# First block: own buffers for the modulation weights, an even split of the convolution taps, and another order of the output projection

## The chip, the cores and the metric

The program runs on one core of a Trainium2 chip. The metric is the device time of one execution in microseconds, and the median of a few executions is compared. The core's engines have a queue each: TensorE (PE, with its weight loads shown apart as PEld), VectorE (DVE), ScalarE (ACT), GpSimd (POOL) and SyncE (SP), which starts the large transfers from memory. Each queue runs in order. What one engine needs from another it waits for at a semaphore.

## The reference, cut to what matters

The program is two networks in a row. Only the first is touched, and a set of vectors that the second needs. The first has two layers over 272 rows (16 meta tokens and 256 tokens) of width 1024:

```
hn = rmsnorm(h, norm1_g[l]);  proj = hn @ w_in[l]          # q, k, v, u
q, k = rope(q), rope(k)
attn = rmsnorm((softmax(q1 k1) - lam * softmax(q2 k2)) @ v, subln_g) * (1 - lam_init)   # 4 heads
z    = a * sigmoid(gate)                                   # a, gate from u + b_glu
conv = silu(layer_norm(depthwise_conv(z, 31 taps) + conv_b))    # 512 channels
h = h + concat(attn, conv) @ w_out[l]
h = h + (silu(gate) * up) @ w_down[l]
```

The second network scales and shifts its rows by modulation vectors, silu(c) @ w_ada + b_ada, of 6 x 1024 values. They depend on no row of the first network, so they may be computed at any time before.

## The kernel before

Activations lie transposed, channels on partitions and rows along the free axis. A weight matrix is read in blocks of 1024 x 256 (1 MB). `weights` (L153) puts a block into one of three `raw` buffers by a transfer from SP's queue, then ACT and DVE split it into a high and a low half (`hi`, `lo`, three buffers each), and `mm3` (L169) takes three products of reduced precision for each 128 x 128 piece.

In each layer `first_block` makes z from four blocks of w_in (L352 to L365), q and k from four more (L372 to L386), v from two (`values`), and then attention, convolution and the output projection. `ORDER` gives the order in which the source lists the steps: scores, values, attention, convolution, part of the modulation (`ada_parts`), the channel norm, and the four blocks of w_out. The source's order is not the order on the engines: a planner with a model of the times lists each engine's instructions, and an earlier place in the source is a higher priority. `high_priority` raises it.

The rows of the attention are cut into three tiles of 16, 128 and 128 rows (two in the second layer, which drops the first). `scores` makes one product for each tile, head and half (L420), adds the mask and takes the maximum on DVE (L421), exponentiates on ACT (L425), and joins the two halves on DVE (L428 to L431). `attention` transposes the weights (L453), multiplies with v (L461), and norms each tile by itself: four squares on ACT (L465), a root, a reciprocal, a product (L470), transposes (L474), and the split into `cat` (L477, L478).

The convolution has 31 taps for each of four groups of 128 channels. `TAPS` says which run on TensorE: in the first layer all 31 of group 0 and 16 of group 1, in the second 16 of group 0. Such a tap needs a diagonal matrix made by ACT (L487) and is one product (L488). The others are one DVE instruction each (L498, L501). `channel_norm` follows, with sigmoid written by Tanh (L521).

The modulation has 24 parts of 256 columns, 12 in the first layer, 10 in the second and 2 after the last w_down (`ADA`). Each takes 1 MB of w_ada through a `raw` buffer (the last two through the buffers `xh` and `xl`, `ada_ahead`), eight products with 32 columns (L630), a copy on ACT (L633) and two products that turn the row (L635). The buffer `bigb` holds `cat` from early in the layer on, and later half of the MLP's activations.

The output projection keeps five accumulators open (`AHEAD`), takes for them the half of w_out that meets the attention first, then the half that meets the convolution.

Of the kernel before, what the change touches and what calls it, by code (L numbers as in the profile page):

```python
# [13 lines left out]
OP = mybir.AluOpType  # L14

# [12 lines left out]
ADA = (12, 10, 2)  # L28
TAPS = (((0, 31), (1, 16)), ((0, 16),))
AHEAD = 5  # L30
PR0 = 9
ORDER = ("svacpnwwww", "svacpnwwww")
# [77 lines left out]
class K:  # L110
# [171 lines left out]
    def first_params(s):  # L282
# [8 lines left out]
        V.tensor_scalar(cw.rearrange("p a b -> p (a b)"), t[:, :248], 0.5, None, op0=OP.mult)  # L291
        lamv = ap.tile([128, 4, 2, 64], F32, name="lamv", tag="vf", bufs=2)
# [13 lines left out]
        return cw, nlam  # L306

    def first_block(s):
# [18 lines left out]
        s.scr, s.row = dict(tag="scr", bufs=3), dict(tag="qraw", bufs=2)  # L327
        s.nsq = dict(tag="sq", bufs=3)
        for l in range(2):
# [18 lines left out]
            cat = (sub(s2, 0, KC), sub(s2, KC * T, KC))  # L348
# [18 lines left out]

# [3 lines left out]
            qk = []  # L371
            for i, (t0, n) in enumerate(((tq, nq), (0, T))):  # L372
                dst = sub(s1, nz + (4 + 4 * i) * T, 4)
                qk.append(dst)
                sl = slice(t0, t0 + n)
                for b in range(2):
                    w = s.weights(w_in, 0, 8, 512 * i + 256 * b)
                    for j, p in enumerate(s.block2([(w, 8, 0)], x, t0, n)):
# [4 lines left out]
                        d = dst[:, 2 * b + j, sl]  # L383
# [3 lines left out]
            q, k = qk  # L387

            if l == 0:
                P.update(s.columns(ap, ap, (("norm2_g", 16), ("conv_b", 8), ("conv_ln_g", 8), ("conv_ln_b", 8),  # L390
                                            ("subln_g", 2)), s.G, tag="scr", bufs=3))
                subg = ap.tile([128, 2], F32, name="subg")
                hlg = ap.tile([128, 8], F32, name="hlg")
                hlb = ap.tile([128, 8], F32, name="hlb")
                for i in range(2):
                    V.tensor_scalar(subg[:, i:i + 1], P["subln_g"][:, i:i + 1], 1.0 - LAM0[i], None, op0=OP.mult)
                V.tensor_scalar(hlg, P["conv_ln_g"], 0.5, None, op0=OP.mult)
                V.tensor_scalar(hlb, P["conv_ln_b"], 0.5, None, op0=OP.mult)
                cw, nlam = s.first_params()
                s.ada()  # L400
            rcs, pro = [], []

            def scores():
                for i, (q0, n) in enumerate(QT):
                    if q0 < tq:
                        continue
                    nk = q0 + n
                    mk = C["mask"][:n, T - 128 - q0:T - 128 + n] if n == 128 else C["mask"][:n, 144:144 + n]
                    st = ap.tile([128, 5, 4, 2], F32, name="st", bufs=3)
                    mx, ng, sm, rc, cf = (st[:n, a] for a in range(5))  # L410
                    prs = []
                    rcs.append(rc)
                    pro.append(prs)
                    for hd in range(4):
                        pr = [ap.tile([128, T], F32, name=f"pr{c}", bufs=(PR0, 3)[c]) for c in range(2)]
                        prs.append(pr[0])
# [6 lines left out]
                        V.tensor_scalar(ng[:, hd], mx[:, hd], -1.0, None, op0=OP.mult)  # L423
                        for c in range(2):
                            A.activation(pr[c][:n, :nk], pr[c][:n, :nk], AF.Exp, bias=ng[:, hd, c:c + 1],  # L425
                                         accum_out=sm[:, hd, c:c + 1])

                        V.reciprocal(rc[:, hd], sm[:, hd])  # L428
                        V.tensor_scalar(cf[:, hd, 0:1], sm[:, hd, 0:1], rc[:, hd, 1:2], nlam[:n, l:l + 1], op0=OP.mult,
                                        op1=OP.mult)  # L430
                        V.scalar_tensor_tensor(pr[0][:n, :nk], pr[1][:n, :nk], cf[:, hd, 0:1], pr[0][:n, :nk],  # L431
                                               op0=OP.mult, op1=OP.add)

            def attention():
                at = [s.ap.tile([128, KC * T], F32, name="at", tag=t) for t in ("xl", "xh")]
                for (i, (q0, n)), rc, prs in zip([(i, t) for i, t in enumerate(QT) if t[0] >= tq], rcs, pro):
# [8 lines left out]
                    for kt, hds, dst in parts:  # L445
# [3 lines left out]
                        for e, hd in enumerate(hds):  # L449
                            for b in range(w):  # L450
                                k0, kn = QT[kt + b]
                                o = 128 * (w * e + b)
                                PE.transpose(pt[:kn, o:o + n], prs[hd][:n, k0:k0 + kn], ident[:n, :n])  # L453
# [3 lines left out]
                    po = s.mm()  # L457
                    ss = ap.tile([128, 4], F32, name="oss", bufs=2)
# [4 lines left out]
                    for hd in range(4):  # L463
# [4 lines left out]
                    V.tensor_tensor(ss[:n], ss[:n], rc[:, :, 0], op=OP.mult)  # L468
                    o3 = ap.tile([128, 4, 128], F32, name="osb", bufs=2)
# [76 lines left out]


            wo = []
            for step in ORDER[l]:
                if step == "a":  # L550
                    attention()
                elif step == "s":
# [1141 lines left out]
```

## Time and profile before

| | |
|---|---|
| median of 3 runs | 1670.59 us (1669.11 to 1671.02) |
| profiled execution, its time | 1669.04 us |
| profiled execution, its span | 1667.2 us |
| PE, PEld busy in the span | 1598.1 us (96%), 1358.0 us (81%) |
| DVE, ACT, POOL busy | 865.5, 744.5, 14.4 us |
| mean granted TensorE clock | 0.984 of full speed |

The span goes from the first to the last instruction, and the 1.84 us around it belong to the time. A busy PE is one with a product in flight; products overlap, so the start of one to the start of the next tells what it costs. The first layer's stages from the projections to the output projection lie at about 20 to 185 us of the span, the second layer's at about 400 to 535 us, and the first network ends at about 741 us.

### The profile page before, as it was taken

To read this page: it belongs to the slowest core of one execution; us is meant where nothing else is said; L and a number is where in the kernel's file an instruction comes from. 1 tells how busy PE (TensorE), PEld (TensorE's weight loads), DVE (VectorE), ACT (ScalarE), POOL (GpSimd) and SP (SyncE) were. 2 spreads that over 40 slices of the span, in tenths; PEclk is the share of its full clock that TensorE was granted. 3 is DMA by queue.
4 is the path that set the end of the run, shared out by engine and by line. 5 is a ranking of instruction groups with operands and counts; after the bars stand their busy time and mean duration, and the time that the engine had idled before them with its cause. 6 is when DMAs were issued, how large, how long until landed. Compare 5 with 4: busy or idle time off the path is not lost.

```text
span 1667.2 us, 32866 instructions
## 1 busy us (share of the span) xinstructions
PE 1598.1 (96%) x13630; PEld 1358.0 (81%) x13630; DVE 865.5 (52%) x1764; ACT 744.5 (45%) x1492; POOL 14.4 (1%) x28
## 2 busy tenths in 40 slices
PE   7999999999999999989999999999899999999897
PEld 6966999999968999988999999999666576566463
DVE  6685766646987666458656654553422221222122
ACT  5376644445347544455856856643322211112121
POOL 2000000000000000000000000000000000000000
PEclk9999999999999999999999999999899999999999
DMA  8408655555466555754343342666799999999995
GB/s 249 140 26 274 194 179 174 172 172 174 130 203 192 176 189 171 234 167 140 114 128 102 102 129 89 233 191 223 285 365 421 420 419 420 420 420 420 420 420 243
DMA packets 209959, 389.29 MB, mean 234 GB/s; under 512 B 8855, under 2 KB 183313, under 8 KB 184977
## 3 DMA queue, kind: packets, MB, share of 16 engines
q1 hardware_dynamic: 209104, 386.66, 64.0%
q8 instruction: 108, 1.77, 0.5%
q0 software_dynamic: 704, 0.51, 0.3%
q14 instruction: 43, 0.34, 0.1%
HBM read 386.10 MB, written 1.05 MB: 232 GB/s over the span
## 4 chain that ended last, share of the span: by engine, by line
PE 76%; DMA 14%; ACT 5%; DVE 4%; issue 1%; SPq 0%; DVEq 0%; ACTq 0%
PE mm L172 14%; PE mm L173 14%; PE mm L174 14%; PE pm L1508 6%; DMA we<-in_w_exp_up 6%; PE pm L1534 4%; DMA we<-in_w_exp_down 3%; DMA we<-in_w_exp_gate 2%; PE pm L1472 2%; PE dx L488 2%; PE mm L195 2%; PE mm L196 1%; PE mm L197 1%; ACT hi L165 1%; DMA raw<-in_w_out 1%; PE dx L630 1%
## 5 line engine op out<-in xcount | busy, mean ns | idle before, releaser
L166 DVE TENSOR_TENSOR lo<-raw,hi 128x1024 fp32r<-128x1024 f32 (+2 forms) x300 | 347.9, 1192 | 144.2 <-ACT hi L165 142.9
L165 ACT CAST hi<-raw 128x1024 fp32r<-128x1024 f32 (+2 forms) x300 | 292.7, 1024 | 271.0 <-PE mm L173 150.5
L172 PE MATMUL mm<-xh,hi 128*128 128x272 f32 (+1 forms) x1008 | 288.1, 288 | 0.0
L173 PE MATMUL mm<-xl,hi 128*128 128x272 f32 (+1 forms) x1008 | 287.8, 286 | 0.0
L174 PE MATMUL mm<-xh,lo 128*128 128x272 f32 (+1 forms) x1008 | 286.6, 286 | 0.0
L1508 PE MATMUL pm<-we,xT 128*32 128x256 f32 (+2 forms) x2048 | 195.9, 392 | 8.4 <-DMA we<-in_w_exp_up 5.8
L173 PEld LDWEIGHTS mm<-xl,hi 128*128 128x128 f32 x1008 | 189.7, 188 | 0.9
L174 PEld LDWEIGHTS mm<-xh,lo 128*128 128x128 f32 x1008 | 189.4, 188 | 0.5
L172 PEld LDWEIGHTS mm<-xh,hi 128*128 128x128 f32 x1008 | 188.5, 188 | 0.7
L1508 PEld LDWEIGHTS pm<-we,xT 128*32 128x32 f32 (+2 forms) x2048 | 122.2, 129 | 76.0 <-DMA we<-in_w_exp_up 7.9
L173 PE MATMUL mm<-bigb,hi 128*128 128x256 f32 (+1 forms) x512 | 148.3, 290 | 0.1
L172 PE MATMUL mm<-hh,hi 128*128 128x256 f32 x384 | 110.6, 291 | 7.2 <-ACT hh L704 4.2
L1534 PE MATMUL pm<-we,hT 128*32 128x512 f32 (+2 forms) x512 | 112.5, 605 | 0.1
L173 PE MATMUL mm<-hl,hi 128*128 128x256 f32 x384 | 109.5, 286 | 0.7 <-DVE hl L705 0.7
L174 PE MATMUL mm<-hh,lo 128*128 128x256 f32 x384 | 108.4, 285 | 0.0
L1519 DVE SCALAR_TENSOR_TENSOR hp<-sil,cs,pm 128x256 f32<-128x256 f32 x26 | 17.6, 676 | 168.5 <-ACT sil L1517 168.5
L174 PE MATMUL mm<-biga,lo 128*128 128x272 f32 (+1 forms) x352 | 101.4, 288 | 0.0
L172 PE MATMUL mm<-biga,hi 128*128 128x272 f32 (+1 forms) x352 | 100.6, 286 | 0.0
L173 PEld LDWEIGHTS mm<-bigb,hi 128*128 128x128 f32 x512 | 97.5, 191 | 0.8 <-DVE bigb L478 0.3
L1539 DVE TENSOR_TENSOR y<-pm,gt 128x512 f32<-128x512 f32 x52 | 35.9, 689 | 119.5 <-PE pm L1534 119.5
L1517 ACT ACTIVATE sil<-pm 128x256 f32<-128x256 f32 x26 | 10.0, 384 | 175.2 <-PE pm L1508 175.2
L195 PE MATMUL mm<-hi,hh 128*128 128x256 f32 x288 | 85.8, 298 | 2.0 <-DVE cacc L861 2.0
(541 smaller groups left out, 3089.7 us busy)
## 6 DMA issues: line engine op xcount, KB each, us to landing
we<-in_w_exp_gate SPq DMA_DIRECT2D x64, 1024.0 KB, 19.6
we<-in_w_exp_up SPq DMA_DIRECT2D x64, 1024.0 KB, 19.8
we<-in_w_exp_down SPq DMA_DIRECT2D x64, 1024.0 KB, 19.7
raw<-in_w_in SPq DMA_DIRECT2D x62, 1024.0 KB, 5.3
raw<-in_w_gate_up SPq DMA_DIRECT2D x44, 1024.0 KB, 5.1
raw<-in_w_ada SPq DMA_DIRECT2D x22, 1024.0 KB, 6.0
raw<-in_w_down SPq DMA_DIRECT2D x16, 1024.0 KB, 5.1
raw<-in_w_out SPq DMA_DIRECT2D x12, 1024.0 KB, 6.7
```

The costliest lines, as they stand in the source:

```text
L165: s.A.copy(hi[:, a:b], raw[:, a:b])
L166: s.V.tensor_tensor(lo[:, a:b], raw[:, a:b], hi[:, a:b].bitcast(F32), op=OP.subtract)
L172: s.PE.matmul(ps[:, :n], a, xh, start=start, stop=False)
L173: s.PE.matmul(ps[:, :n], a, xl, start=False, stop=False)
L174: s.PE.matmul(ps[:, :n], b, xh, start=False, stop=stop)
L195: s.PE.matmul(p[:, :256], xh, w[0][:, k], start=(k == 0), stop=False)
L488: PE.matmul(p[:, :nq], dg, z[:, c, tq + j:tq + j + nq], start=(j == 0), stop=(j == n - 1))
L1472: s.PE.matmul(p[:, 256 * kk:256 * kk + 256], s.ht[h][:, i, k + kk], oh[:, i], start=(i == 0 and h == 0), stop=(i == 1 and h == 1))
L1508: mm = PE.matmul(gu[sg, 256 * m:256 * m + 256], xT[:, k, o + sg.start:o + sg.stop], w[m][:, k], start=(k == 0), stop=(k == 7))
L1519: V.scalar_tensor_tensor(hp.rearrange("p k q -> p q k"), sil.rearrange("p (q k) -> p q k", k=2), cs, gu[:, 256:].rearrange("p (q k) -> p q ...
L1534: PE.matmul(py[sg], hT[:, k, sg], w[2][:, k, 512 * j:512 * j + 512], start=(k == 0), stop=(k == 1))
L1539: V.tensor_tensor(y, py, s.gt2[:, 512 * j:512 * j + 512], op=OP.mult)
```

## The change

The modulation's weights no longer use the `raw` ring. `ada_parts` cuts `bigb` into three buffers of 1 MB, for which SP's transfers are listed without a raised priority, and `cat` takes `bigb` afterwards. The parts are 13 and 11, none after the last layer. The source lists, in each layer: q and k, modulation, convolution, values, scores (for two heads at a time), channel norm, attention, w_out. The convolution takes 31 taps on TensorE in both layers. Parameters of the convolution and the modulation's vectors are made before z. The scores of two heads share their small DVE instructions; the attention's tiles share one root, at the end, and take their squares in one ACT instruction and a DVE sum. The channel norm uses Silu in place of Tanh and four more operations per group. Five accumulators of the output projection begin with the convolution's half.

```diff
-ADA = (12, 10, 2)
-TAPS = (((0, 31), (1, 16)), ((0, 16),))
-ORDER = ("svacpnwwww", "svacpnwwww")
+ADA = (13, 11)
+TAPS = (((0, 31),), ((0, 31),))
...
             if l == 0:
+                P.update(s.columns(ap, ap, (("norm2_g", 16), ("conv_b", 8), ("conv_ln_g", 8), ("conv_ln_b", 8),
+                                            ("subln_g", 2)), s.G, tag="scr", bufs=3))
+                cw = s.first_params()
+                s.ada()
                 C.update(s.consts(ap, 1))
...
-            s2 = s.big(1, F32R, (2 * KC * T,))
...
+                    V.tensor_scalar(ng[:, hs], mx[:, hs], -1.0, None, op0=OP.mult)
+                    for hd in (2 * b, 2 * b + 1):
                         for c in range(2):
+                            pr = prs[i, hd][c][:n, :nk]
+                            A.activation(pr, pr, AF.Exp, bias=ng[:, hd, c:c + 1], accum_out=sm[:, hd, c:c + 1])
...
-                    for hd in range(4):
-                        scr = ap.tile([128, 128], F32, name="scr", bufs=3)
-                        A.activation(scr[:n], po[:n, 128 * hd:128 * hd + 128], AF.Square, scale=rc[:, hd, 0:1],
-                                     accum_out=ss[:n, hd:hd + 1])
-                    s.rsqrt(ss[:n], ss[:n], s.eps5, 1.0 / 128)
...
+                    A.activation(sq[:n], po[:n], AF.Square)
+                    V.tensor_reduce(oss[:n, i], sq[:n].rearrange("p (a b) -> p a b", b=128), axis=AX.X, op=OP.add)
+                    V.tensor_tensor(oss[:n, i], oss[:n, i], st[:n, i, 5, :, 0], op=OP.mult)
+                i0 = tiles[0][0]
+                s.rsqrt(oss[:, i0:], oss[:, i0:], s.eps5, 1.0 / 128)
+                for i, q0, n in tiles:
...
-                    A.activation(th[:, :nq], acc[:, c, :nq], AF.Tanh, bias=hlb[:, i:i + 1], scale=hlg[:, i:i + 1])
...
+                    A.activation(a, a, AF.Silu, bias=P["conv_ln_b"][:, i:i + 1], scale=P["conv_ln_g"][:, i:i + 1])
...
+            for b in range(2):
+                rotated(b)
+            s.ada_parts(ADA[l])
+            conv()
+            values()
+            for b in range(2):
+                scores(b)
+            s2 = s.big(1, F32R, (2 * KC * T,))
+            cat = (sub(s2, 0, KC), sub(s2, KC * T, KC))
+            channel_norm()
+            attention()
+            wo = [s.weights(I["w_out"][l], 0, 8, 256 * b) for b in range(4)]
...
             for j in range(AHEAD):
-                for k_ in range(4):
-                    s.mm3(ps[j], wo[j // 2], k_, 128 * (j % 2), cat, k_, tq, nq, k_ == 0, False)
+                for k_ in range(4, KC):
+                    s.mm3(ps[j], wo[j // 2], k_, 128 * (j % 2), cat, k_, tq, nq, k_ == 4, False)
...
-        s.ada_parts(ADA[2], wada)
...
-    def ada_parts(s, n, ws=()):
+    def ada_parts(s, n):
...
+        ws = s.big(1).rearrange("p (a k f) -> p a k f", a=3, k=KC)
         for i in range(s.nada, s.nada + n):
-            w = ws[i - s.nada] if ws else s.weights(s.I["w_ada_2"][0], 0, 8, 256 * i, False)
+            w = ws[:, i % 3]
+            s.SP.dma_start(w, dap(src, 256 * i, [[ld, 128], [128 * ld, KC], [1, 256]]))
```

## Rows read from the trace of the kernel before

**Rows 1.** The page's first part: busy time of each engine, share, instructions.

```profile
PE 1598.1 (96%) x13630; PEld 1358.0 (81%) x13630; DVE 865.5 (52%) x1764; ACT 744.5 (45%) x1492; POOL 14.4 (1%) x28
```

**Rows 2.** Stretches of the first block: length, busy PE, PEld, DVE, ACT, POOL, clock, DMA.

```profile
40.00:78.00 38.00, 38.00 (x290) 37.05 (x290) 23.86 (x41) 14.24 (x23) 0.00 (x0) 1.00 0.50 167
78.00:120.00 42.00, 42.00 (x224) 28.54 (x224) 35.58 (x152) 27.57 (x92) 0.00 (x0) 1.00 0.02 5
120.00:158.00 38.00, 37.03 (x317) 25.30 (x319) 22.62 (x64) 22.35 (x73) 0.00 (x0) 1.00 0.75 244
...
405.00:470.00 65.00, 65.00 (x486) 60.82 (x485) 61.51 (x143) 26.78 (x51) 0.00 (x0) 1.00 0.35 114
470.00:500.00 30.00, 26.57 (x250) 15.99 (x249) 24.51 (x99) 15.80 (x53) 1.10 (x2) 1.00 0.89 280
500.00:517.00 17.00, 13.35 (x65) 10.15 (x65) 13.53 (x20) 13.15 (x27) 0.00 (x0) 0.90 0.97 311
...
160.74:170.42 9.68, 9.44 (x47) 7.83 (x48) 6.04 (x10) 8.09 (x15) 0.00 (x0) 0.50 0.94 295
```

**Rows 3.** PE in order of time at the first layer's output projection: start, length.

```profile
160.74 1.93 PE L630 MATMUL dx<-raw,cs 128*32 128x256 f32 x16 [1.99 <-DMA raw<-in_w_ada]
```

**Rows 4.** SP's queue, 60 to 165 us: in total, times, longest.

```profile
SPq L158 <- PE dx L630: 84.0, 11, 47.1
```

**Rows 5.** Transfers issued from 78 to 120 us, then from 470 to 510: count, size, landing.

```profile
raw<-in_w_ada SPq DMA_DIRECT2D x1, 1024.0 KB, 5.2
...
raw<-in_w_ada SPq DMA_DIRECT2D x7, 1024.0 KB, 7.6
```

**Rows 6.** What PE waited for, 405 to 517 us: total, times, longest.

```profile
PE mm L474 <- DVE osb L470: 2.1, 2, 1.1
```

**Rows 7.** Chain that ended last, pieces of PE: start, length (an f32 product is x2).

```profile
89.03 2.03 PE dx L488 x8
91.21 0.66 PE dx L488 x2
...
108.68 0.65 PE ax L420 x2
...
116.87 1.00 PE dx L630 x16
...
141.69 0.54 PE dx L635 x4
...
450.22 1.73 PE dx L488 x8
...
475.43 0.66 PE ax L420 x4
...
170.96 0.12 PE mm L173
```

**Rows 8.** DVE's groups from 78 to 165 us, then one from 405 to 517.

```profile
L501 DVE SCALAR_TENSOR_TENSOR biga<-biga,cw 128x272 f32<-128x272 f32 x75 | 35.4, 491 | 0.3
L421 DVE CUSTOM_DVE_ANT_0 pr<-ax,blob 16x16 f32<-16x16 f32 (+2 forms) x24 | 7.0, 298 | 4.5 <-PE ax L420 4.1
L431 DVE SCALAR_TENSOR_TENSOR pr<-pr,st,pr 16x16 f32<-16x16 f32 (+2 forms) x12 | 4.3, 359 | 0.0
L429 DVE TENSOR_SCALAR st<-st,nlam 128x1 f32<-128x1 f32 (+1 forms) x12 | 3.2, 263 | 0.0
L470 DVE TENSOR_TENSOR osb<-mm,oss 128x512 f32<-128x512 f32 (+1 forms) x3 | 2.1, 685 | 0.1
...
L501 DVE SCALAR_TENSOR_TENSOR biga<-biga,cw 128x256 f32<-128x256 f32 x105 | 47.2, 478 | 0.1
```

**Rows 9.** ACT in order of time: two table loads of the second layer.

```profile
407.49 1.28 ACT L363 ACT_TABLE_LOAD   x1
...
496.71 1.28 ACT L201 ACT_TABLE_LOAD   x1
```

**Rows 10.** End of the first block: the copies of two parts on ACT.

```profile
739.22 0.61 ACT L633 COPY adarow<-dx 128x256 f32<-128x256 f32 x2
```

More of the change, by code (lines that the diff above doesn't have):

```diff
@@ L370, in first_block, with rotated @@
             V.tensor_tensor(srs, C["sin"], r, op=OP.mult)
[L371 to L376, printed above, removed]
+            q, k = sub(s1, nz + 4 * T, 4), sub(s1, nz + 8 * T, 4)
+            def rotated(b):
+                for i, (t0, n) in enumerate(((tq, nq), (0, T))):
+                    sl = slice(t0, t0 + n)
                     w = s.weights(w_in, 0, 8, 512 * i + 256 * b)
@@ L396, in first_block @@
                     V.tensor_scalar(subg[:, i:i + 1], P["subln_g"][:, i:i + 1], 1.0 - LAM0[i], None, op0=OP.mult)
[L397 to L406, printed above, removed]
+                nlam = s.first_lambda()
@@ L407, in scores @@
+            tiles = [(i, q0, n) for i, (q0, n) in enumerate(QT) if q0 >= tq]
+            st = ap.tile([128, 3, 6, 4, 2], F32, name="st")
+            oss = ap.tile([128, 3, 4], F32, name="oss")
+            V.memset(oss, 1.0)
+            prs = {}
+            def scores(b):
+                hs = slice(2 * b, 2 * b + 2)
+                for i, q0, n in tiles:
                     nk = q0 + n
                     mk = C["mask"][:n, T - 128 - q0:T - 128 + n] if n == 128 else C["mask"][:n, 144:144 + n]
-                    st = ap.tile([128, 5, 4, 2], F32, name="st", bufs=3)
@@ L422, in scores @@
                                                    mx[:, hd, c:c + 1])
-                        V.tensor_scalar(ng[:, hd], mx[:, hd], -1.0, None, op0=OP.mult)
+                    V.tensor_scalar(ng[:, hs], mx[:, hs], -1.0, None, op0=OP.mult)
+                    for hd in (2 * b, 2 * b + 1):
                         for c in range(2):
[L425 to L432, printed above, removed]
+                            pr = prs[i, hd][c][:n, :nk]
+                            A.activation(pr, pr, AF.Exp, bias=ng[:, hd, c:c + 1], accum_out=sm[:, hd, c:c + 1])
+                    V.reciprocal(rc[:, hs], sm[:, hs])
+                    V.scalar_tensor_tensor(cf[:, hs, 0], sm[:, hs, 0], nlam[:n, l:l + 1], rc[:, hs, 1], op0=OP.mult,
+                                           op1=OP.mult)
+                    V.tensor_tensor(r2[:, hs, 0], rc[:, hs, 0], rc[:, hs, 0], op=OP.mult)
+                    for hd in (2 * b, 2 * b + 1):
+                        p0, p1 = (t[:n, :nk] for t in prs[i, hd])
+                        V.scalar_tensor_tensor(p0, p1, cf[:, hd, 0:1], p0, op0=OP.mult, op1=OP.add)
             def attention():
-                at = [s.ap.tile([128, KC * T], F32, name="at", tag=t) for t in ("xl", "xh")]
-                for (i, (q0, n)), rc, prs in zip([(i, t) for i, t in enumerate(QT) if t[0] >= tq], rcs, pro):
+                at = [ap.tile([128, KC * T], F32, name="at", tag=t) for t in ("xl", "xh")]
+                out = {}
+                for i, q0, n in tiles:
                     a0 = at[i // 2]
@@ L545, in values @@
                         A.copy(v[:n, i, 256 * b:256 * b + 256], p[:n, :256])
[L548 to L552, printed above, removed]
-                    scores()
-                elif step == "v":
-                    values()
-                elif step == "c":
-                    conv()
-                elif step == "n":
-                    channel_norm()
-                elif step == "w":
-                    wo.append(s.weights(I["w_out"][l], 0, 8, 256 * len(wo)))
-                else:
-                    s.ada_parts(ADA[l])
+            for b in range(2):
[10 more added lines that the diff above has]
+            wo = [s.weights(I["w_out"][l], 0, 8, 256 * b) for b in range(4)]
             h1 = s.hp.tile([128, KC, T], F32, name="h", bufs=2)
@@ L571, in first_block @@
                     ps.append(s.mm())
-                for k_ in range(4 if j < AHEAD else 0, KC):
-                    s.mm3(ps[j], wo[j // 2], k_, 128 * (j % 2), cat, k_, tq, nq, k_ == 0, k_ == KC - 1)
+                for k_ in range(-4 if j >= AHEAD else 0, 4):
+                    s.mm3(ps[j], wo[j // 2], k_ % KC, 128 * (j % 2), cat, k_ % KC, tq, nq, k_ == -4, k_ == 3)
                 V.tensor_tensor(h1[:, j, tq:], ps[j][:, :nq], h[:, j, tq:], op=OP.add)
@@ L669, in mixer @@
         C, C2, ident = s.C, s.C2, s.C["ident"]
-        s.scr = s.row = s.nsq = dict(tag="sc", bufs=6)
-        if not hasattr(s, "mod"):
-            s.ada()
-            s.ada_parts(24)
-            s.mix_begin()
-            s.hg = s.hp.tile([128, KC, T], F32, name="hg", tag="h", bufs=2)
-            for k in range(KC):
-                s.mix_tile(s.h, s.hg, k)
+        s.scr = s.nsq = dict(tag="sc", bufs=6)
         P, mod, h = s.P2, s.mod, s.h
```

75 lines of the change are left out of this document (30 added, 45 removed).

## The prediction

> **What bounds the kernel now.** I read the page's engine shares first. PE is busy for 96% of the span, DVE for 52%, ACT for 45% [rows 1]. Shares hide stages, so next came the stretches of the first block. From 40 to 120 us PE is busy for all of both stretches, and so it is from 405 to 470 [rows 2]; what is saved there must be saved in PE's work. PE falls behind in three places: 0.97 us idle from 120 to 158, 3.43 us from 470 to 500, 3.65 us from 500 to 517 [rows 2]. The order of time on PE shows a fourth, at the first layer's output projection: a wait of 1.99 us for a block of w_ada [rows 3]. Behind it the granted clock is 0.50, the 1.2 GHz level, for 9.68 us [rows 2]; at the full level that work takes half, so 4.84 us go there. From 500 to 517 the clock is 0.90, which costs 1.7 us.
>
> So the first layer loses 0.97 + 1.99 + 4.84 = 7.8 us and the second 3.43 + 3.65 + 1.7 = 8.8 us. This is less than the chain of waits suggests, since PE does other work while a transfer is named there.
>
> Why the losses arise: DMA is at 0.02 from 78 to 120 us, then at 0.75, and at 0.89 to 0.97 from 470 to 517 [rows 2]. SP's queue stood 84.0 us for the modulation's products, once 47.1 us [rows 4]: a modulation block holds a raw buffer until PE takes it, and what stands behind it in SP's queue, w_out at last, waits too. In the second layer seven blocks of w_ada are issued in 40 us and land after 7.6 us [rows 5]. The longest other wait there is for the norm of the attention on DVE, 2.1 us [rows 6].
>
> **The change part by part.** *Own buffers.* Three modulation blocks can be loaded from the time bigb is free, while PE makes q and k, and DMA is half idle from 40 to 78 and idle to 120 [rows 2]. w_out meets only blocks of w_in in the raw ring. I take all 7.8 and 8.8 us as removed; the bound on the other side is that half of them returns as waits elsewhere, 8.3 us. If an early modulation load is listed ahead of a block of w_in on SP's queue, that block lands later; PE has three split blocks ahead, so I count nothing, and where that cover is gone the price is one landing, 7.6 us at most [rows 5].
>
> *Taps.* Four taps in a row cost PE 2.03 us in the first layer, a first load and 0.46 us each, and 1.73 us, 0.43 each, in the second [rows 7]. The first layer loses 16 taps on PE, -7.4 us; the second gains 15, +6.5 us. On DVE a tap is 35.4 / 75 = 0.47 us in the first and 47.2 / 105 = 0.45 us in the second layer [rows 8]: 16 more are +7.5 us, 15 fewer -6.7 us. The first layer's are hidden: its parameters now come before z, and DVE is free for 38.0 - 23.9 = 14.1 us from 40 to 78 [rows 2], where no tap could run before. Without that cover they would end 7.5 us later, still before PE's other work. The transposes and small POOL loads of these parameters only move; POOL is busy for 1% [rows 1].
>
> *Parts.* One part costs PE 1.00 us for its products and 0.54 us to turn the row [rows 7], so one more in each layer is +1.5 us. The two at the end of the block lay in PE's wait for the last sums, and cost the chain there only their copies on ACT, 0.61 us [rows 10]; I take -0.5 us.
>
> *Order and grouping.* One tap alone costs 0.66 us, four in a row 0.51 us each; one score product alone costs 0.65 us, and a pair, in two halves of the rows, 0.66 us together [rows 7]. In the first layer the eight large score products run alone. If half of them pair and some taps gather, this is -2 us; the bounds are 0 and -5 us (all eight paired, 2.6 us, and sixteen taps by 0.15). The second layer pairs already: 0.
>
> *A new tail.* Modulation, convolution and values now stand ahead of the scores in the source, so PE spends its fillers first. At the end all tiles share one root: table load 1.28 us [rows 9], Square and sum by the nearest row of the same size, 2 x 0.69 us, three products of 0.69 us (two in the second layer), and the transposes and split by two rows more of that kind, about 6.1 us in the first layer [rows 8]. Before, the modulation's last parts lay under such a tail. Now only the convolution's half of w_out does, on the two accumulators that do not share banks with the attention: 2 x 12 products of 0.12 us, 3 us [rows 7]. I take +3 us for each layer; the bounds are 0, with more banks free in time, and 6 us. The small DVE operations saved in the scores (L429's 3.2 us fall to about half [rows 8]) stay off PE's path while PE is full; where it is not, they are a part of rival B.
>
> Sum: first layer -7.8 - 7.4 + 1.5 - 2 + 3 = -12.7; second layer -8.8 + 6.5 + 1.5 + 0 + 3 = +2.2; end -0.5; together -11.0 us. Against the profiled execution, 1669.04 us, this gives 1658.0 us. The median of the runs is 1.55 us above that execution, so I forecast 1659.5 us; the gain comes from the first layer, and the second breaks even.
>
> **The rivals.** *A. It packs without a tail.* No tail, the grouping at its bound: -7.8 - 7.4 + 1.5 - 5 = -18.7, -0.8 in the second layer, -0.5: 1650.6 us. For it: w_out's first half can run in the tail; against it: its other accumulators wait for the attention's banks.
>
> *B. PE starves in the scores (slower).* The scores' DVE work is 7.0 + 4.3 + at most 3.2 = 14.5 us in the first layer [rows 8], against eight pairs of products, 5.3 us [rows 7]. If the fillers are gone when they begin, PE idles 9.2 us there and two thirds of it, 6.1 us, in the second layer, which has two tiles in place of three, and the clock falls as it did after 1.99 us of waiting, 4.8 us: 1659.5 + 20.1 = 1680 us. It decides from the point where the fillers end before DVE's taps do. Fillers: 13 x 1.54 + 31 x 0.46 + values, 96 products of 0.12, = 46 us, from about 77 to 123. DVE's taps: 93 x 0.47 = 44 us, 14 of them done by 78, so to about 108. That leaves 15 us of cover for 14.5 us of scores: narrowly enough.
>
> *C. New DMA waits.* Three blocks in flight with 7.6 us each [rows 5] make a part every 2.5 us; if PE's list wants them after the 5.2 us of a lone load [rows 5], each turn of three buffers is 2.4 us late, eight turns in both layers, 19 us at most. PE stood for a block of w_ada for 1.99 us before [rows 3]. I price half: 1669 us.
>
> *D. Table loads.* Tanh gives way to Silu, and the channel norm now ends while exps are still to come. The second layer's exps ran on the table loaded for Tanh at 407.49, and its root needed a load at 496.71 [rows 9]. Exp, Sqrt, Silu, Exp, Sqrt in turn would be four more loads in a layer, 8 x 1.28 = 10.3 us if the tail waits for all: 1670 us. Against it: ACT is busy for 66% and 59% of the stretches from 78 to 158 [rows 2], so most would hide. The Trainium skill (ScalarE: Activation LUTs, section Table sets: the hidden batching unit) gives the rule that speaks against this part: batch activation calls by table set; exp and tanh share one, exp and sqrt do not. By that rule, the two loads of rows 9 and the exps between them agree. The same page (section What ACT_TABLE_LOAD costs) puts a switch at about 2.66 us with the drain, by which rival D would be an estimated 21 us; the trace shows 1.28 us for the load itself.
>
> *E. Nothing.* The tail takes what the waits gave: 1668 to 1672 us.
>
> **How the numbers follow.** Forecast 0.44, A 0.18, B 0.13, C 0.12, D 0.08, E 0.05. The likeliest is 1659.5 us, its own range 1653 to 1666. For 8 in 10 the range reaches to A and D and leaves out B and the ends: 1647 to 1672 us. A measurement of this kernel tells 0.2%, 3.3 us, from no change, so faster is below 1667.2 and slower above 1673.9. Faster: forecast, A, half of C and a little of D, 0.70. Same: half of C, most of D, E, 0.17. Slower: B, 0.13.
>
> **What the profile after would show.** Right: w_ada loads from about 20 us on, DMA well above 0.02 from 78 to 120; no wait of PE for w_out or w_ada over 1 us; 62 taps on PE; clock 1.00 at both output projections; the first layer's MLP begins some 10 to 15 us earlier, the second layer's length stays within 5 us. Wrong: PE idle over 5 us between the projections and w_out in either layer, with DVE or ACT named (B, D), or with w_ada named (C); or more than three table loads in a layer's middle. What would make it wrong most easily is the planner's list, which cannot be seen before.

## The result and the profile after

The changed kernel takes 1693.93 us (median of 4, 1691.77 to 1695.77) against 1670.80 us: ratio 1.0138, 95% interval 1.0118 to 1.0158, so it is slower by 1.4%. The forecast was 1659.5 us and its range ended at 1672. One kernel below, e2, fell into two groups, 1675 us in four executions and 1689 to 1693 us in five; its profiles are of the upper one.

The profiled execution took 1693.76 us, its span is 1692.0 us, 24.8 us more than before. The two layers, each from the first product of its norm to the first of its MLP's norm, before and then after; columns as in [rows 2]:

```profile
18.33:180.57 162.24, 159.04 (x1115) 129.79 (x1115) 115.28 (x311) 95.78 (x236) 1.60 (x3) 0.97 0.52 169
369.33:528.76 159.43, 152.34 (x1171) 133.76 (x1169) 123.27 (x295) 79.37 (x169) 1.10 (x2) 0.99 0.54 172
```
```profile
19.32:185.01 165.69, 155.04 (x1099) 126.37 (x1099) 118.06 (x314) 83.05 (x192) 1.62 (x3) 0.92 0.53 170
374.80:548.82 174.02, 162.36 (x1219) 142.98 (x1218) 116.31 (x272) 80.55 (x166) 1.11 (x2) 0.95 0.52 164
```

The first layer is 3.5 us longer, the second 14.6. The first starts 1.0 us later and its MLP takes 1.0 us more; the second's takes the same, so the last sum of w_down ends at 756.1 us in place of 736.0. Behind it the other network takes 4.8 us more. The sum is 24.9.

Each layer can be cut in three: PE's idle time (length less busy), what the clock costs ((1 - clock) x length), and the rest, which is PE's work at the full clock. The work comes out low where PE idles at half clock, since such a time counts one and a half times:

```
              first layer                   second layer
           length  idle  clock  work     length  idle  clock  work
before      162.2   3.2    4.9  154.2     159.4   7.1    1.6  150.7
after       165.7  10.7   13.3  141.8     174.0  11.7    8.7  153.7
```

The clock is read to two digits, so an entry under clock or work is good to 0.8 us. And runs below that give PE the same products differ by some 7 us under work (138.5 in e1 to 145.6 in e3 in the first layer, 150.8 in h1 to 157.8 in e3 in the second), because that column also holds how the products are grouped and what idles at half clock. A difference of a few us in it tells nothing by itself.

So the work went the way that the sum had it: -12.4 us in the first layer, where -7.9 was forecast, and +3.0 in the second, where +8.0 was. Idle time and clock were to go from 8.1 and 8.7 us to some 3 each; they went to 24.0 and 20.4. Over the whole span the mean granted clock fell from 0.984 to 0.973, which is about 19 of the 24.8 us.

Where: stretches that answer to [rows 2], and PE's waits in the first and the second layer (total, times, longest):

```profile
78.00:120.00 42.00, 38.74 (x336) 28.95 (x336) 34.62 (x95) 12.31 (x26) 0.00 (x0) 0.88 0.94 301
120.00:158.00 38.00, 38.00 (x189) 25.15 (x186) 19.64 (x92) 25.95 (x91) 0.00 (x0) 0.87 0.01 1
158.00:175.00 17.00, 10.77 (x55) 8.89 (x54) 10.85 (x26) 11.03 (x22) 0.00 (x0) 0.80 0.00 0
470.00:500.00 30.00, 25.75 (x194) 19.20 (x194) 24.84 (x85) 10.74 (x33) 0.00 (x0) 0.77 0.61 178
517.00:540.00 23.00, 16.08 (x84) 13.69 (x84) 10.12 (x22) 13.36 (x28) 0.00 (x0) 0.93 0.00 1
...
113.28:130.85 17.57, 17.04 (x83) 9.42 (x82) 12.34 (x53) 6.40 (x23) 0.00 (x0) 0.52 0.31 99
```
```profile
PE mm L171 <- ACT bigb L527: 4.3, 1, 4.3
PE dx L628 <- DVE st L420: 2.4, 1, 2.4
PE dx L519 <- ACT sq L518: 1.7, 1, 1.7
...
PE mm L171 <- ACT bigb L527: 4.2, 1, 4.2
PE dx L628 <- DMA bigb<-in_w_ada: 3.5, 1, 3.5
PE mm L478 <- DVE osb L474: 1.6, 1, 1.6
```

And PE in order of time in the first layer (L628 and L633 a modulation part, L419 scores, L492 taps, L463 weights times v, L511 and L519 the channel norm, L478 the attention's output, L171 w_out):

```profile
108.31 0.59 PE L419 MATMUL ax<-biga 64*16 64x16 f32 x6
111.34 1.07 PE L628 MATMUL dx<-bigb,cs 128*32 128x256 f32 x4 [2.44 <-DVE st L420]
112.34 1.01 PE L633 MATMUL dx<-sel,adarow 128*128 128x1 f32 x4
113.28 1.92 PE L628 MATMUL dx<-bigb,cs 128*32 128x256 f32 x12
...
117.61 1.93 PE L628 MATMUL dx<-bigb,cs 128*32 128x256 f32 x16
...
127.61 3.32 PE L492 MATMUL dx<-biga,dg 128*128 128x272 f32 x8
...
134.86 2.10 PE L492 MATMUL dx<-biga,dg 128*128 128x272 f32 x8
...
157.28 1.66 PE L463 MATMUL ax<-biga,at 128*128 128x128 f32 x10
158.78 2.00 PE L511 MATMUL dx<-biga,blob 128*128 128x272 f32 x8
162.46 2.10 PE L519 MATMUL dx<-sq,blob 128*128 128x272 f32 x8 [1.69 <-ACT sq L518]
164.50 1.00 PE L478 MATMUL mm<-blob,osb 16*128 16x16 f32 x8
165.70 0.66 PE L478 MATMUL mm<-blob,osb 128*128 128x128 f32 x4 [0.20 <-DVE osb L474]
170.70 1.05 PE L171 MATMUL mm<-bigb,hi 128*128 128x272 f32 x3 [4.34 <-ACT bigb L527]
```

The reader is to see three things. PE stands 2.44 us at 109, and from 113 to 131 us the granted clock is 0.52: sixteen products of a part take 1.93 us in place of 1.00 [rows 7], until taps have run for some 3 us. The first tap comes at 127.6, when the modulation is done; at 89.0 before [rows 7]. And the convolution ends last, its channel norm follows the attention, and w_out, which begins with the convolution's half, waits for just that: for the table load, Silu and cast that end ACT's chain:

```profile
167.10 1.28 ACT L525 ACT_TABLE_LOAD   x1
169.22 1.12 ACT L525 ACTIVATE biga<-biga,pc_norm_g 128x272 f32<-128x272 f32 x2 [0.84 <-DVE biga L524]
170.24 0.40 ACT L527 CAST bigb<-biga 128x272 fp32r<-128x272 f32 x1
```

At the end of the block, where two parts stood before [rows 10], PE waits 2.28 us for the squares, and the sums behind them run at half clock (0.53 from 757.9 to 761.5 us, 1.00 before). The first products of the next network run at half clock too, but they did so before; the third line is of the kernel before:

```profile
757.91 3.58 PE L650 MATMUL ax<-nsq,blob 128*128 128x256 f32 x8 [2.28 <-ACT nsq L649]
766.02 1.01 PE L171 MATMUL mm<-hh,hi 128*128 128x256 f32 x3 [4.53 <-ACT hh L684]
...
745.48 1.01 PE L172 MATMUL mm<-hh,hi 128*128 128x256 f32 x3 [4.18 <-ACT hh L704]
```

That product comes 9.9 us after the last sum of w_down, and 9.5 before. So this wait and this clock explain some 0.4 of the 4.8 us that the other network takes more.

### The profile page after: what moved, and what is told of

Read it like the earlier page. It is cut to its first block, busy times and chain, and to the rows that moved or that the text cites. A ratio compares the mean times of both kernels' runs of the same rounds, so it can differ in the third digit from the quotient of the medians.

```text
span 1692.0 us, 32796 instructions
## 1 busy us (share of the span) xinstructions
PE 1603.7 (95%) x13628; PEld 1363.9 (81%) x13628; DVE 861.5 (51%) x1744; ACT 736.2 (44%) x1445; POOL 14.5 (1%) x28
## 4 chain that ended last, share of the span: by engine, by line
PE 78%; DMA 11%; ACT 6%; DVE 4%; issue 1%; SPq 0%; ACTq 0%; DVEq 0%
PE mm L171 14%; PE mm L172 14%; PE mm L173 14%; PE pm L1488 8%; DMA we<-in_w_exp_up 7%; PE pm L1514 4%; PE pm L1452 2%; DMA we<-in_w_exp_down 2%; PE dx L492 2%; PE dx L628 1%; PE mm L194 1%; PE mm L195 1%; PE mm L196 1%; ACT hi L164 1%; PE ax L463 1%; PE ax L419 1%
## 5 line engine op out<-in xcount | busy, mean ns | idle before, releaser
L171 PE MATMUL mm<-xh,hi 128*128 128x272 f32 (+1 forms) x1008 | 290.0, 290 | 0.2 <-DVE a L366 0.2
L171 PEld LDWEIGHTS mm<-xh,hi 128*128 128x128 f32 x1008 | 189.0, 188 | 3.1 <-issue 1.2
L171 PE MATMUL mm<-hh,hi 128*128 128x256 f32 x384 | 110.7, 292 | 7.3 <-ACT hh L684 4.5
L171 PE MATMUL mm<-biga,hi 128*128 128x272 f32 (+1 forms) x352 | 100.6, 286 | 0.0
```

Source lines behind the costliest of these rows:

```text
L171: s.PE.matmul(ps[:, :n], a, xh, start=start, stop=False)
```

## The experiments

The theories, as they stood before the first run: 1, taps and modulation parts share the two dx banks in the order of the source, so the taps stand behind parts that transfers pace, and the convolution ends last; 2, 31 taps are too many for TensorE in the second layer; 3, the convolution's half of w_out is the wrong one to begin with; 4, the early transfers take bandwidth from w_in. Theory 5, the order of the source, came later.

All runs in the terms above, each from one profiled execution: median, then for each layer length, idle, clock, work; the end of the last w_down sum; what follows it in the span. The kernel before, run again beside them, had medians of 1668.9 to 1670.8 us. Five profiles lie off their kernel's median: e1 (1715.8 us), h1 (1709.4) and e2 (1693.3) above it, h3 (1688.5) and e5 (1696.6) below. e7 alone leaves values out. Behind the block the second network then runs products (L1610 to L1646 of its kernel, behind 1300 us) that the changed kernel does not run at all, so only its layers are compared.

```
                  us      first layer              second layer             sum at  behind
before        1670.6  162.2  3.2  4.9 154.2   159.4  7.1  1.6 150.7   736.0   931.1
after         1693.9  165.7 10.7 13.3 141.8   174.0 11.7  8.7 153.7   756.1   935.9
e3            1689.8  161.8  6.6  9.7 145.6   168.5  7.3  3.4 157.8   745.9   941.3
e6 (before)   1687.5  165.3  7.3  3.3 154.7   164.7  9.7  6.6 148.4   745.4   941.8
e7            1859.8  163.3  9.9  8.2 145.2   172.2 10.0  5.2 157.0   752.2       -
e1            1707.1  172.7 10.1 24.2 138.5   181.2  9.3 16.3 155.5   770.5   943.6
e2            1689.2  169.1  5.6 22.0 141.5   173.3  5.6 13.9 153.9   758.0   933.6
e2 again      1693.0  168.6  5.3 21.9 141.4   176.2  5.6 17.6 153.0   760.9   930.4
h1            1695.5  170.5  9.2 20.5 140.9   181.6  9.0 21.8 150.8   769.2   938.4
k1            1694.6  159.0  5.2 12.7 141.1   171.8  7.4  8.6 155.8   746.5   947.5
e5 (before)   1701.3  161.9 13.7  6.5 141.7   175.7  9.9 10.5 155.3   753.9   940.9
g3 (before)   1692.4  172.8 20.6 15.6 136.7   163.0  6.6  3.3 153.2   749.0   944.1
f1            1691.8  160.9  8.1  8.0 144.7   170.9 10.4 12.0 148.6   746.5   942.1
g1            1702.5  181.1 10.0 14.5 156.6   168.2  1.9 11.8 154.5   759.7   941.3
g2 (before)   1750.0  197.1 23.6 31.5 142.0   192.0 19.2 30.7 142.0   805.7   944.1
g4            1697.7  168.5 14.7 10.1 143.7   168.3  6.0  5.0 157.2   753.3   941.4
f4            1695.8  160.5  8.2  8.0 144.3   167.4 10.9 10.0 146.4   744.6   949.4
h3            1699.0  160.5 11.2  8.0 141.3   175.4  8.8 15.8 150.8   752.0   934.7
k3            1699.5  161.0 10.6  9.7 140.8   177.3  8.9 16.0 152.4   753.7   945.4
h4 (before)   1687.9  166.7  4.1  6.7 156.0   166.8  8.2 10.0 148.6   745.2   941.8
```

**Which half of w_out first (e3, e6).** e3 undoes the order of the halves in the changed kernel; e6 makes the change's edit alone, in the kernel before.

```diff
-                for k_ in range(4, KC):
+                for k_ in range(4):
```

> The changed kernel, but the five open accumulators of w_out begin with the half that meets the attention, as in the kernel before. Theory 3 (the order of the halves is the cause): 1668 to 1676 us. Theory 1: the convolution still ends last and the attention's own norm ends only some 4 to 9 us before it, so a wait of 4.3 us and the slow clock behind it, some 2 us, go in each layer at most: 1681 to 1692 us.

> The kernel before with the convolution's half of w_out first and nothing else. If that half is the better cover for a tail (my prediction's reading), the waits for the attention's norm shrink: 1666 to 1670 us. If it is the half that comes last (theory 3, which took 3.8 us from the first and 5.5 us from the second layer when undone in the changed kernel): 1673 to 1681 us.

e3 ends the block 10.2 us earlier (3.9 and 5.5 us in the layers), e6 9.4 us later (3.1 and 5.3 us). The two agree. The lengths alone would not show it, since h4, below, touches no half and ends the block 9.2 us later as well. What shows it are the waits: e6 has the wait of the changed kernel, in its first and then its second layer, and in e3 the wait ahead of w_out is short in both:

```profile
PE mm L172 <- ACT bigb L526: 4.1, 1, 4.1
...
PE mm L172 <- ACT bigb L526: 5.5, 1, 5.5
```
```profile
PE dx L171 <- ACT bigb L481: 0.8, 1, 0.8
...
PE mm L171 <- ACT bigb L481: 0.9, 1, 0.9
```

So the half is worth 10.2 of the 20.1 us by the end of the block, and 6.8 of these are the two waits (4.3 and 4.2 us, now 0.8 and 0.9). In time e3 returns only 4.1 us, though, for what follows the block takes 5.4 us more. e6 pays 10.7 us there, in code that no edit touches. In the 64 us behind the last sum, PE's waits before and in e6:

```profile
PE mm L172 <- ACT hh L704: 4.2, 1, 4.2
PE mm L195 <- DVE cacc L861: 1.5, 1, 1.5
PE mm L172 <- DVE cacc L861: 1.2, 1, 1.2
```
```profile
PE mm L172 <- ACT hh L704: 4.2, 1, 4.2
PE mm L172 <- DVE cacc L861: 3.5, 2, 3.2
PE mm L195 <- DVE cacc L861: 1.5, 1, 1.5
```

The engines' orders in that stage differ as well (ACT's from some 25 us behind the sum on). Most of the edits below paid something of this kind against the 931.1 us of the kernel before, up to 18.3 us (f4); e2 paid at most 2.5.

**The transfers (e7).** Only the first three parts of each layer are loaded.

```diff
-            s.SP.dma_start(w, ...)
+            if i - s.nada < 3:
+                s.SP.dma_start(w, ...)
```

> The changed kernel without the modulation's transfers after the first three of each layer: the other parts multiply what lies in the three buffers, so the modulation's values are left out from there on, while every product on PE remains. Theory 1 says that the transfers pace the parts and these the taps: without them the parts pass early, the taps start before 100 us, and the time is 1655 to 1675 us. Theory 4 says the same of the time, but not of the swap of two lines, which moves no transfer. Theories 2 and 3: PE's work and the order of the halves are as they were, 1685 to 1694 us.

The layers shrink by 2.4 and 1.8 us. The wait of 2.44 us is gone, so it was a transfer's, though the profile names DVE. The first tap still comes at 123.7 us, where theory 1 had it before 100: the transfers are a small part, and theory 4 has these 4.2 us at most.

```profile
123.66 2.63 PE L492 MATMUL dx<-biga,dg 128*128 128x272 f32 x5
```

**Taps behind parts (e1, e2, k1, h1).** In the changed kernel taps and parts take turns on two dx banks in the order of the source. e1 swaps the two lines; e2 gives the parts a bank of their own; k1 adds a priority for the copies of the rows to e2; h1 is e2 with the attention's half first.

```diff
-            s.ada_parts(ADA[l])
             conv()
+            s.ada_parts(ADA[l])
```
```diff
-            p = s.dx()
+            p = s.dy()
...
+            with s.tc.high_priority(offset=300):
                 A.copy(row, p[:, :256])
```

> The changed kernel with two source lines swapped: the convolution is listed ahead of the modulation. Theory 1 (convolution taps on TensorE and modulation parts share the two dx banks, which are handed out in source order, so the taps stand behind parts that the transfers pace, and convolution and channel norm end last): the taps start before 80 us in place of 127.6, PE waits for the channel norm's output under 1.5 us in place of 4.3, and most of the 23 us comes back, 1662 to 1674 us. Theory 2 (31 taps on TensorE in the second layer are too many): PE has the same work, so 1688 to 1694. Theory 3 (the convolution's half of w_out first is the wrong order): the half waits for the channel norm all the same, 1682 to 1690. Theory 4 (early modulation transfers take bandwidth from w_in): unchanged, 1690 to 1695.

> The changed kernel with its source order kept, but one of the two dx banks belongs to the modulation alone, the other to convolution and channel norm. Theory 1: it is the bank that couples them, so this does as much as the swap of the two lines, within 4 us of it, 1662 to 1676 us, with taps on PE before 80 us. Rival within theory 1 (the place in the source, as a priority, holds the taps back, not the bank): taps still start after 115 us and the time stays at 1688 to 1696. Theories 2 to 4: 1688 to 1695.

> The changed kernel with a bank for the modulation alone, once more, for a profile. If it falls into the faster group (1675 us): the same instructions in the same order, and the difference of some 17 us lies where the slower profile had the clock at 0.50 to 0.57 (from 140 to 180 us and from 500 to 540 us), with no other wait gone. If it falls into the slower group again, that stays open.

> The changed kernel with the bank for the modulation alone and the attention's half of w_out first. If bank and half are the loss and add up: the own bank gave 18 us in its faster group (1675), the half 4 us of time and 10 us by the end of the block, so 1663 to 1671 us. If the convolution's half, which is ready early here, is the better cover (the prediction's reading), the half undone costs time: 1675 to 1695 us in either group.

> The changed kernel with a bank for the modulation alone, and the copy and turn of a modulation row at a priority raised by 300. If TensorE's wait of 2.10 us for this copy starts the stretch at half the clock (47 us long in the first layer): no wait for it over 0.6 us, clock 1.00 in all of 100 to 160 us, and all runs at 1665 to 1680 us. If the clock falls for want of wide products between the thin ones of the modulation, whatever is waited for: clock under 0.8 in 120 to 160 us and the time at 1685 to 1700 us.

The bank does couple them: in e1 and e2 the taps run from 48 us on in place of 127.6. As the cause of the loss theory 1 falls in e1 (1707.1 us, where it had 1662 to 1674). In e2 it stays open. Four executions took 1675.0 to 1676.0 us, inside its range, and five took 1689.2 to 1693.3; the repetition took 1693.0, so there is no profile near 1675. But the granted clock of each execution is on record: 0.978 or 0.979 over the span in the four, which costs 35 to 37 us, and 0.963 to 0.966 in the five, 57 to 63 us. So the clock accounts for the 17 us between them, and where it holds, the own bank takes back 18 to 19 of the 23 us.

In the profiles (e1 at 1715.8 us, e2 at 1693.3) parts are what is left for the end (their products run until 159 us in e1, 170 in e2), and the clock goes. A long stretch of e2 with the wait ahead of it, and the same of k1:

```profile
131.08 0.61 PE L639 MATMUL dy<-sel,adarow 128*128 128x1 f32 x4 [2.10 <-ACT adarow L637]
...
131.08:177.50 46.42, 44.60 (x218) 30.04 (x219) 18.53 (x79) 23.21 (x56) 0.00 (x0) 0.52 0.15 47
```
```profile
135.78 1.02 PE L640 MATMUL dy<-sel,adarow 128*128 128x1 f32 x4 [2.99 <-ACT adarow L638]
...
133.00:163.00 30.00, 26.44 (x135) 16.59 (x136) 12.89 (x51) 17.38 (x47) 0.00 (x0) 0.60 0.11 36
```

PE is busy for 96% of 46 us at half the clock. The clock fell after a wait of 2.10 us for the copy of a row and rose some 6 us into w_out. k1 did not take the wait away (2.99 us remain, behind exps on ACT). Its time and its clock (0.89 from 120 to 140 us, 0.52 from 140 to 160) are those of its second reading, but with the wait still there the run does not separate the two. Its stretch at half clock is shorter; its first layer, 159.0 us, is the shortest of all, and its time is lost in the second layer and behind the block. In h1 bank and half do not add up (1695.5 us, where 1663 to 1671 was the sum). h1 against e2 turns e3 round: where the convolution is early, its half looks the better one to begin with, by 1.4 to 1.9 us in the first layer and 5.4 to 8.3 in the second. This is a hint only, since h1's profile is of its longest execution (1709 us; the others 1692 to 1699).

**The split of the taps (e5, g3, f1).** e5 puts the new split into the kernel before; g3 puts there 31 and 16 taps, with the parameters made before z; f1 is e3 with 16 taps in the second layer.

```diff
-TAPS = (((0, 31), (1, 16)), ((0, 16),))
+TAPS = (((0, 31),), ((0, 31),))      # e5
+TAPS = (((0, 31),), ((0, 16),))      # g3, f1
```

> The kernel before with the changed kernel's split of the taps alone: 31 on TensorE in each layer. My terms: -7.4 us in the first layer, +6.5 us in the second, so 1666 to 1672 us. Theory 2 in its new form: the second layer loses 7 to 9 us, while the first gains less than 7.4 us, since DVE gets 16 taps more (7.5 us) late in the stage: 1672 to 1682 us.

> The kernel before with 31 taps on TensorE in the first layer in place of 47, and the convolution's parameters and the modulation's vectors made before z, so that DVE can begin its taps early. My term of -7.4 us is right if the first layer shrinks from 162.2 us by 5 to 8 us. It is wrong if TensorE stands idle in place of the taps, as it did for 13.7 us in the run with 31 and 31: then the first layer stays within 2 us of 162.

> The changed kernel with the attention's half of w_out first (as in the run before this one) and, in the second layer, 16 taps on TensorE in place of 31. Theory 2 in its new form (in the second layer TensorE had no room for 15 more taps; they cost it 9.1 us there, 16.7 against 7.6): the second layer's length falls by 7 to 9 us from 168.5 us and the first stays at 161.9; the time is 1680 to 1683 us. Rival (DVE's taps, 0.45 us each, would then end last): DVE gets 6.7 us more, conv ends no earlier, and the time stays within 3 us of 1690.

Without 16 taps the first layer's work falls by 12.5 us in e5 and 17.5 in g3, more than the 7.4 us of the taps, as far as that column can tell. Its length falls by 0.3 us in e5 and grows by 10.6 in g3. PE in g3:

```profile
147.92 0.61 PE L640 MATMUL dx<-sel,adarow 128*128 128x1 f32 x4 [0.30 <-ACT adarow L638]
160.23 1.11 PE L479 MATMUL mm<-blob,osb 128*128 128x128 f32 x4 [11.70 <-DVE osb L475]
161.14 2.88 PE L458 MATMUL mm<-blob,pr 128*16 128x128 f32 x12
163.94 7.56 PE L466 MATMUL mm<-biga,at 16*128 16x128 f32 x24
```

The last part ends at 148.5. What is left on PE, the third tile's transposes and products (L458, L466), stands in its list behind the second tile's output (L479), which waits for the attention's norm, so nothing fills that wait. DVE's taps are not late, the last came at 122. But the norm's small steps stand on DVE between the splits of w_out and the channel norm: the root ends at 150.7 on ACT, the product (L475) begins at 159.5. So it looks to be the order of both lists that costs, with the fillers gone; no run tests this. In the second layer 15 taps more cost e5 16.3 us: 4.6 of work, 11.7 of idle time and clock. Taking them back in f1 saves 9.2 us of work and loses 11.7: DVE's last tap moves from 492 to 519 us, and PE waits 3.4 us for it:

```profile
PE dx L511 <- DVE biga L505: 3.4, 1, 3.4
```

**The order of the source, and the norm (g1, g2, g4).** g2 is the kernel before with the new order; g1 is f1 with the old taps in the first layer too and the old order; g4 is e3 with a root for each tile.

```diff
-ORDER = ("svacpnwwww", "svacpnwwww")
+ORDER = ("pcvsnawwww", "pcvsnawwww")      # g2
```

> The kernel before with the changed kernel's source order alone: modulation, convolution, values, scores, channel norm, attention, in both layers; raw ring, taps, halves of w_out as before. Theory 5: this order alone makes each layer 3 to 10 us longer, the last w_down sum at 742 to 756 us. Rival: order matters only together with the split of the taps, the last sum within 3 us of 736.

> The changed kernel with the old split of the taps, the attention's half of w_out first, and in the source scores, values, convolution, modulation (as before) in place of modulation, convolution, values, scores. Own buffers, shared small operations, one root and Silu stay. Theory 5 (what is left of the loss lies in the source's order: scores listed last come too late, and their chain over DVE and ACT ends the stage): the last w_down sum comes back from 745.9 to 733 to 738 us (736.0 before). Rival (own buffers, or the shared root and Silu, cost it): it stays above 742 us.

> The changed kernel with the attention's half of w_out first and the attention's norm of before: four squares on ACT with their sums, and a root for each tile by itself, in place of one root at the end. If the shared root makes a tail (my term of +3 us for each layer), the last w_down sum comes 2 to 8 us before the 745.9 us of the run with the shared root. If the tail is the convolution's, it stays within 1.5 us.

With the raw ring the new order costs g2 34.9 and 32.6 us: the parts run first (81 to 117 us), scores only from 150 us on, and in the first layer PE waits 8.8 us for the attention's norm and 6.6 for w_ada. This is the side that theory 5 had, and far more than its 3 to 10 us. In g1 the block ends at 759.7 us, where theory 5 had 733 to 738: the parts come last instead, and the attention, whose output needs bigb, waits for them; what its shared norm costs cannot be read there. In g4 the first layer is 6.7 us longer, the second 0.2 us shorter than in e3: the shared root is no tail that a root for each tile would avoid.

**Parts at the end, a bank for the kernel before (f4, h3, k3, h4).** f4, h3, k3 are f1, h1, k1 with `ADA = (12, 10, 2)`; k3 has the convolution's half first, h3 the attention's. h4 is the kernel before with the bank of e2.

> The kernel of the run before it with 12, 10 and 2 modulation parts: the last two again at the end of the first block, through xh and xl. If these two parts had kept TensorE busy over its wait for the last squares (2.28 us in the changed kernel, 0.42 us before) and so at the full clock into the next stage, the time falls by 1.5 to 5 us against that run, most of it after the last w_down sum: 1676 to 1681 us. If they only moved (my prediction counted 0.5 us for their removal as a gain), the time is within 1.5 us of that run or 0.5 us above it.

> The run before it with 12, 10 and 2 modulation parts, the last two at the end of the block again. By the rows of the changed kernel (2.28 us of waiting for the last squares, and products at half the clock behind it) they are worth 2 to 4 us against that run, and one part less in each layer 1 to 2 us more. If the list of the next stage decides, as in the earlier run with end parts (which gained 2 us by the end of the block and lost 7 us behind it), it is slower than that run.

> The run before it with 12, 10 and 2 modulation parts, the last two at the end of the first block. If the terms add (one part of 1.5 us less in each layer, TensorE's wait for the last squares covered): 3 to 6 us faster than that run. If lists decide: within 10 us of it on either side, and not below 1669 us.

> The kernel before with a bank for the modulation alone and nothing else. There the convolution is listed ahead of the modulation, so taps do not stand behind parts: within 4 us of 1670. If the shared bank costs the kernel before as well, 1655 to 1665 us; if its list falls apart like those of the other single edits, 1680 to 1700 us.

f4 ends the block 1.9 us earlier and loses 7.3 behind it. By their medians f4, h3 and k3 are slower than f1, h1 and k1, by 4.0, 3.5 and 4.9 us, where 1.5 to 6 us were forecast as gains; h3's executions overlap with h1's. None of the three tells what the two parts are worth, for each has lists of its own.

h4 was to stay within 4 us of 1670 and takes 1687.9. It ends the block 9.2 us later and pays 10.7 behind it, with the taps and the halves as they were. So every edit tried on the kernel before cost 17 us or more (e6, h4, g3, e5, g2), even the one that only hands out two banks in another way. That leaves a rival that no run rules out: the kernel before may have lists that any edit worsens, and a part of each loss may be this and not the edit named. No version has a median below 1687 us; e2's four executions at 1675 came nearest.

## Why the prediction was wrong

- **Bound.** PE bounds, as read. But its list was read as work that could shrink. Work fell by 9.4 us in the two layers (forecast: -7.9 in the first, +8.0 in the second, near nothing in all); idle time and clock rose by 27.6.
- **Own buffers.** The step that failed: "I take all 7.8 and 8.8 us as removed", with half of it as the bound. In place of falling by these, idle time and clock rose by 15.9 us in the first layer and 11.7 in the second. The losses did not go with the raw ring. The transfers do go early (DMA 0.94 from 78 to 120 us), but PE waits for a part all the same, 2.44 and 3.5 us, and for the convolution's half of w_out, 4.3 and 4.2 us. "I count nothing" for early loads ahead of w_in held: from 17 to 110 us PE waits 0.7 us for a split block and 0.2 us for z.
- **Taps.** A tap costs what [rows 7] say (2.10 us for four; 2.03 before), and the first layer's work did fall. It is not a saving in time: e5 gives up 16 taps for 0.3 us, g3 for a loss. That DVE's taps are hidden was right in the first layer, but they end at 133.4 us and not at 108; PE's own taps end at 157.4.
- **Order and tail.** In the +3 us for each layer the 3 us of cover were mis-signed: the convolution's half was counted as cover and was the last thing to come. It cost 3.9 and 5.5 us (e3), 3.1 and 5.3 alone (e6). That these lie near +3 is luck: the term was for the attention's shared root, and a root for each tile gained nothing (g4). With the convolution early the reading may hold (h1 against e2).
- **End.** -0.5 us forecast, +4.8 measured behind the last sum. The wait of 2.28 us and the half clock behind it make 0.4 of it by the next network's first product; the rest is not taken apart. That lists behind the block change, by up to 18 us, had no term at all, and the range was too narrow by it.
- **Rivals.** B had the side, and the kind: PE starves and its clock falls. Its place was wrong. The scores had cover, the taps from 127 to 157 us; PE starved at the parts before them and at the norms behind. Its price, 20.1 us over the forecast, stands against 34.4. C is worth 4.2 us by e7. D is out: there are three table loads from 78 us on in the first layer, where four were before, and four in the second as before. Two of 1.28 us lie in the first layer's tail (at 159.6 and 167.1), one did before (158.0).
- **Signs.** Right were 31 taps in each layer, the early loads, DMA from 78 to 120. Wrong were the clock at both projections, no wait for w_ada over 1 us (2.44 and 3.5), the MLP 10 to 15 us earlier (4.4 later), the second layer within 5 us (14.6).

Open: the halves of w_out account for half of the 20.1 us by the end of the block, in both directions. With the half undone (e3) the other half is nearly all in the second layer (168.5 us, 159.4 before). By the table 7.1 of these 9.1 us are work, near the +8.0 that the sum had for 15 taps and a part. But taking the taps back (f1) turned it into waiting, for there the convolution ended last on DVE. No edit undone gave this half back in a profile, and e2's four executions at 1675 us, which may have, were not profiled. So the cause of the rest of the loss stays open, between the shared bank with the clock behind it, the tap split and lists that any edit worsens.

## What to carry to other kernels

Cut a stage into idle time, clock and work before an edit is priced: work that fills the wait for another engine's chain may be worth nothing when it is taken away, as 16 taps were here (e5, g3), and PE's idle time can cost the clock too. Begin an accumulation with the half that the trace shows to be ready first, and look again after every edit that moves either. Where a planner lists the engines from a model, an edit also draws new lists for stages it does not touch, and a price without a bound for that is too sure.

## What the runs showed of the hardware

The granted clock can stay at half, the 1.2 GHz level, while TensorE is busy: 0.52 over 46.4 us with 44.6 us busy (e2). PE ran there products with 32 columns of weights or one column of data (the parts), transposes, scores, the attention's weights times v, and at last w_out. The clock fell at or behind waits of 1.99 us [rows 2, 3], 2.44 us (after), 2.10 us (e2) and 2.99 us (k1). It rose some 3 us into the taps (after) and some 6 us into w_out (e2), but in k1 at 159 us, among products of the attention's weights with v. What decides between these the runs do not tell. The same kernel can come out on either side: e2's executions have a mean clock of 0.978 to 0.979 or of 0.963 to 0.966, 17 us apart.

A switch of ScalarE's tables took 1.28 us of load and nothing more that shows: in the kernel before the square root at 130.40 us begins 1.31 us after the instruction ahead of the load ends:

```profile
128.41 0.68 ACT L487 ACTIVATE dg<-blob,cw 128x128 f32<-128x128 f32 x2
129.10 1.28 ACT L201 ACT_TABLE_LOAD   x1
130.40 0.30 ACT L201 ACTIVATE oss<-oss,eps 16x4 f32<-16x4 f32 x1
```
